# Row adds issued behind GpSimd's gate sums, and a root refined ahead of a gather, in a two-layer encoder

## Chip, cores and metric

One core of a Trainium2 chip runs the whole kernel. The metric is the device time of one execution in microseconds (us). Engines: PE is TensorE, DVE is VectorE, ACT is ScalarE, POOL is GpSimd, SP is SyncE.

## The reference, cut to what matters

Two post-norm encoder layers over 512 tokens of 1024 channels, in float32. Per layer: one input projection for two attention mixers and two sigmoid gates; each mixer's output is projected and weighted with its gate; the gated sum goes through an output projection; then a layer norm of the residual, an MLP with squared ReLU and a gated embedding, and a second layer norm.

```python
DEPTH = 2; DEEPNORM_ALPHA = (2 * DEPTH) ** 0.25
# mixer, at its end
ga, gb = jnp.split(sigmoid(gl + b_gate), 2, axis=-1)
h = einsum('bsd,de->bse', ga * ya + gb * yb, w_out)
# layer
x = layer_norm(DEEPNORM_ALPHA * x + h, ln1_g, ln1_b)
mlp = einsum('bsf,fd->bsd', square(relu(einsum('bsd,df->bsf', x, w_up))), w_down)
ple = sigmoid(einsum('bsd,de->bse', x, w_ple_gate) + b_ple_gate) * einsum('bsr,rd->bsd', p[i], w_ple)
x = layer_norm(DEEPNORM_ALPHA * x + mlp + ple, ln2_g, ln2_b)
# layer_norm(x, g, b) = (x - mean) * rsqrt(var + 1e-5) * g + b
```

## The kernel before

**Products.** A float32 factor is split into a high and a low part (`split`: ACT casts, DVE subtracts), and a product is three matmuls. Weights come packed in blocks of 512 KB from HBM through SP's queue into three staging tiles (`wst`), and are split into `whi` and `wlo` some steps ahead of PE. Line 262 is ACT's cast of all these splits and line 263 DVE's subtraction, so groups of these lines are told apart by tile.

**Gates of the second mixer, and the output projection (layer l).** For u = 0 to 3 and n = 0, 1 the loop at line 1363 takes the gate's tile t = u + 4n: PE computes the gate's projection (24 matmuls, tile `ps_('g', 1, t)`) and the branch's (6 matmuls, `yb`), ACT applies tanh (line 994), and `merged` adds: DVE forms gate times branch (line 1378), then GpSimd adds the first mixer's share (line 1380; at u = 3 DVE does it) into `hr`, of which there is one tile for all u. `mixed` splits the sum (tiles `a11h`, `axh` and their low parts), and behind n = 1 `combine` and `summed` form four more sums on DVE and split them (`smh`, `sml`). Step (u, n) below is one turn of this loop. The output projection (`Out`) and the MLP's second product (`Down`) use Strassen-like products: seven products of sums of blocks, numbered 0 to 6, each in two halves of tokens s = 0, 1; `half` is a half's 12 matmuls and `gather` adds their PSUM tile (`dn...`) into y on DVE. The sums of raw weight blocks (`raw1o`) are partly DVE's, partly accumulating DMAs issued by GpSimd (line 1260).

**The residual.** y[0] to y[3] are four tiles of 128 tokens x 1024 channels. In the second layer they are loaded from `kept` in HBM, on SP's queue (line 1370, one at each u), where the first layer left its normalised values without the norm's bias. The bias row is added afterwards by `add_row` (line 1119): a DMA issued by GpSimd that reads the row from HBM for all 128 partitions and accumulates into y[a]. It has to wait until y[a] has landed.

**Order.** PE's order is written by hand in these places. From the end of the loop (`inner`, line 1394) DVE's and ACT's is too. Elsewhere the program's scheduler orders each engine's instructions by its own forecast of when they become ready; `tc.issue_after(ins)` puts what is issued inside it behind `ins` on that engine, and `recent(engine)` is the newest instruction of that engine in the program's text. GpSimd's order is the scheduler's throughout; each engine runs its instructions in order, and one that waits holds what is behind it.

**The last norm.** In the second layer's last quarter of the MLP (q = 3) PE runs product 4, 5 and 6 by halves. `taken(n, s)` is `half` and `gather`; `moments` takes statistics of a half of y[a] (line 1011, DVE); `roots(a)` aggregates them and starts a root: a reciprocal on DVE, the square root on ACT (line 1040). What it returns, `rest()`, refines the root on DVE (four passes of one column, lines 1048 to 1075) and has ACT centre and scale y[a] (line 1078). `weighed(a)` multiplies by the norm's weight on GpSimd (line 1679) and adds y[a] to `out[a]`, where the bias row lies already, by an accumulating DMA (line 1680). out[2] is turned on PE, scaled on ACT into z and sent by SP (line 1699); out[3] is finished on DVE and sent in three pieces by SP and ACT (line 1738).

Of the kernel before, what the change touches and what calls it, by code (L numbers as in the profile page):

```python
# [17 lines left out]
DVE = mybir.EngineType.DVE  # L18
ACT = mybir.EngineType.Activation
SP = mybir.EngineType.SP  # L20

P = 128
S = 512
# [212 lines left out]
def build(nc, tc, plan, down, xw, xN, pT, wst, vec, rows, sink, cst, out):  # L236
# [3 lines left out]
    with ctx:  # L240
# [4 lines left out]
        def bank(tag, name):  # L245
            return pp.tile([P, 512], F32, tag=tag, name=name, bufs={"mm": 3, "s": 2, "pt": 2, "o": 1}[tag])
# [24 lines left out]
        def recent(engine):  # L271
            return next(i for i in reversed(nc.cur_bb.bb.instructions) if i.engine == engine)

        def in_turn(l):

            return tc.issue_after(recent(SP)) if l else ExitStack()

# [43 lines left out]
        def weights(key, look=LOOK, further=0):  # L321
            c = at[0]
            assert plan[c][0] == key, (plan[c][0], key)
            at[0] += 1
            ahead(c + look, c + further)
            return ready.pop(c)

        def mm3(ps, w, i, x, start, stop, part=False):
            s = slice(i * P, (i + 1) * P)
            nc.tensor.matmul(ps, w[0][:, s], x[0], start=start, stop=False, skip_group_check=part)  # L330
            nc.tensor.matmul(ps, w[0][:, s], x[1], start=False, stop=False, skip_group_check=part)  # L331
            nc.tensor.matmul(ps, w[1][:, s], x[0], start=False, stop=stop, skip_group_check=part)  # L332
# [59 lines left out]
        def load_vectors():  # L392
            with tc.issue_after(recent(SP)):
                nc.sync.dma_start(vraws, vec)
            nc.vector.tensor_scalar(vhs, vraws[:, :, 0:16], 0.5, None, ALU.mult)
# [595 lines left out]
        def gate(l, b, t, vt, rp, ps=None, look=LOOK):  # L991
            ps = linear((l, ("g", b, t)), X, look=look) if ps is None else ps
            g = rp.tile([P, S], F32, tag=f"gate{b}", name=f"gate{l}_{b}_{t}", bufs=2 if b else 8)
            nc.scalar.activation(g, ps, AF.Tanh, bias=vt["half"][:, b * 8 + t:b * 8 + t + 1], scale=0.5)
            return g


        class Tokens:
# [89 lines left out]
            def weighed(self, a, h):  # L1088
                c = h if isinstance(h, slice) else slice(h * 512, (h + 1) * 512)
                nc.vector.scalar_tensor_tensor(self.y[a][:, c], self.y[a][:, c], self.mv[:, a, 0:1], self.g[:, c],  # L1090
                                               ALU.subtract, ALU.mult)
# [26 lines left out]
        def add_row(y, l, i):  # L1118
            nc.gpsimd.dma_start(y, rows[l, i].partition_broadcast(P), accum_op=ALU.add)


        class Down:
# [77 lines left out]
            def product(self, q, n, then=None):  # L1200
                for s in range(2):
                    last = self.gather(q, n, s, self.half(q, n, s))
                    if then:
                        with tc.issue_after(last.ins):
                            then(s)
                return last
# [129 lines left out]
        for l in range(DEPTH):  # L1336
# [18 lines left out]
            y = [yp.tile([P, D], F32, tag=f"y{a}", name=f"y{l}_{a}", bufs=1) for a in range(4)]  # L1355
# [7 lines left out]
            for u in range(4):  # L1363
                hr = mt.tile([P, 4, 256], F32, tag="hr", name=f"hr{l}o{u}", bufs=1)
                for n, t in enumerate((u, u + 4)):
                    g = gate(l, 1, t, vt, mt, look=LOOK if u < 3 else 1 - n)
                    if not n:
                        w = weights((l, ("bb", u)), LOOK if u < 3 else 1)
                        with in_turn(l):
                            nc.sync.dma_start(y[u], kept[u] if l else xN[u])  # L1370
                        if l and u:
                            add_row(y[u - 1], l - 1, 4)
                    ps = bank("mm", f"yb{l}_{t}")
                    for i in range(2):
                        mm3(ps, w, n * 2 + i, OB[i], i == 0, i == 1)

                    def merged(u=u, n=n, t=t, g=g, ps=ps, hr=hr):
                        nc.vector.scalar_tensor_tensor(g, g, 1.0, ps, ALU.add, ALU.mult)
                        h = hr[:, 2 - 2 * n:4 - 2 * n].rearrange("p s t -> p (s t)")
                        (nc.vector if u == 3 else nc.gpsimd).tensor_tensor(h, g, ga[t], ALU.add)  # L1380
                        out7.mixed(hr, u, n)

                    if (u, n) == (3, 1):
                        break
                    merged()
                    if n:
                        out7.combine(hr)
                        out7.summed(hr, u)
                    for step in BESIDE.get((u, n), ()):
                        getattr(out7, step[0])(*step[1:])  # L1390
            manual = ExitStack()
# [5 lines left out]
            out7.cut(2, 0)  # L1397
            out7.add(3, 0)
            out7.combine(hr)
            if l:  # L1400
                add_row(y[3], l - 1, 4)
            mt_close()
            rp_close()
            np1, np1_close = pool(f"np{l}", "right")
# [4 lines left out]
            tn = Tokens(np1, y, f"n1_{l}", LN_EPS / ALPHA ** 2)  # L1409
# [39 lines left out]
            ps = product(1, 0)  # L1449
# [4 lines left out]
            ps = product(1, 1)  # L1454
# [15 lines left out]
            ps = product(4, 0)  # L1470
# [6 lines left out]
            ps = product(4, 1)  # L1477
# [5 lines left out]
            ps = product(3, 0)  # L1483
# [29 lines left out]
            ps = product(6, 0)  # L1513
# [82 lines left out]
            dn = Down(l, qp, hp, y)  # L1596
            dn.operands()
            tn = Tokens(qp, y, f"n2_{l}")
            with tc.manual_schedule(engines={PE}):
                for q in range(FQ):  # L1600
                    for i, m in enumerate(UP_ORDER):
# [3 lines left out]
                        ps = bank("mm", f"ps_up{l}_{q}_{m}")  # L1605
# [58 lines left out]
            q = FQ - 1  # L1664
            with tc.manual_schedule(engines={PE, DVE, ACT}):
                dn.cut(q, 6, 0)
                if last:
# [6 lines left out]
                    def taken(n, s, *cols):  # L1674
                        dn.gather(q, n, s, dn.half(q, n, s, *cols), *cols)
# [25 lines left out]
                    def roots(a):  # L1701
                        return tn.in_two(a, 1, root=True, centre=False)
# [8 lines left out]
                    taken(4, 1)  # L1711
                    tn.moments(1, 1)
                    rest = roots(1)
                    taken(6, 0)
                    tn.moments(2, 0)
                    rest()
                    weighed(1)
                    for n, h in ((5, 2), (6, 0)):
                        for i in range(2):
                            taken(n, 1, i * 256, i * 256 + 256)  # L1720
                            tn.moments(3, h + i, 4)
                            if h + i == 2:
                                rest = roots(2)
                            if h + i == 3:
                                rest()
# [96 lines left out]
```

## Time and profile before

| | us |
|---|---|
| median of 3 runs | 1491.35 |
| the three runs | 1489.59, 1491.35, 1491.5 |
| the profiled execution | 1491.91 |
| its span, first to last instruction | 1490.1 |
| PE busy in it | 1479.2 |
| DVE, ACT, POOL busy in it | 1074.9, 776.5, 253.8 |
| granted TensorE clock, mean | 0.998 |

The profile is of one execution. Times in it count from the span's start. A timeline's row has start, duration, engine, line, operation, out<-in, shapes, count, and in brackets the idle time of the engine before it with what ended it; a row of waits has the total, the number and the longest; the chain is the work that ended last, followed back, each step with its start and duration. In the rows by stretches each engine has its busy time and its instructions, and at the end stand the granted clock, the DMA engines' busy share and GB/s. PEld is PE's weight load, POOLq, ACTq and SPq are the engines' sequencers, q0 is the queue of GpSimd's DMAs, q1 that of SP's, q10 that of ACT's.

### The profile page before, as it was taken

The page shows a single profiled execution, that of the slowest core. Times are in us where ns is not written, and L with a number is a line of the kernel's source. Part 1 is how long each engine was busy: PE and PEld are TensorE (multiplying, and loading weights), DVE is VectorE, ACT ScalarE, POOL GpSimd, SP SyncE. Part 2 cuts the span into 40 slices and gives each one's busy share as a digit, 9 for nine tenths or more (in the row PEclk, how much of TensorE's full clock was granted, in tenths as well). Part 3 has the DMA queues.
Part 4 walks back from the last instruction along what each step waited for, and adds up shares of the span by engine and source line. Part 5 has one row for each costly group of instructions (what it writes and reads, how often), then busy time and mean ns, then how long its engine had stood idle before and what let it go on. Part 6 is the DMA issues. An engine that isn't in the chain of part 4 may idle for free.

```text
span 1490.1 us, 19508 instructions
## 1 busy us (share of the span) xinstructions
PE 1479.2 (99%) x7194; PEld 1232.3 (83%) x7194; DVE 1074.9 (72%) x1859; ACT 776.5 (52%) x1275; POOL 253.8 (17%) x223
## 2 busy tenths in 40 slices
PE   9999999999999999999999999999999999999997
PEld 8888888888888888888888888888788888888886
DVE  6766675789578777676877666756795877777768
ACT  5777764446244344444458777744462544444344
POOL 1212211110021111202012122112110202111021
PEclk9999999999999999999999999999999999999999
DMA  7656564656443414142456666548674433241503
GB/s 248 142 137 154 135 160 124 254 128 162 149 156 101 126 50 152 46 150 71 109 179 144 140 149 143 155 135 252 172 184 142 154 113 114 85 127 44 169 1 99
DMA packets 59759, 203.18 MB, mean 136 GB/s; under 512 B 7408, under 2 KB 7952, under 8 KB 59664
## 3 DMA queue, kind: packets, MB, share of 16 engines
q1 hardware_dynamic: 47120, 159.25, 32.9%
q0 software_dynamic: 11840, 42.47, 15.4%
q8 instruction: 56, 0.92, 0.2%
q10 hardware_dynamic: 704, 0.22, 0.1%
q14 instruction: 39, 0.32, 0.1%
HBM read 160.42 MB, written 6.37 MB: 112 GB/s over the span
## 4 chain that ended last, share of the span: by engine, by line
PE 90%; DVE 4%; ACT 2%; DMA 2%; issue 1%; POOL 1%; SPq 0%; DVEq 0%; POOLq 0%; ACTq 0%
PE dn L1223 20%; PE ps_up L331 8%; PE ps_up L332 8%; PE ps_up L330 8%; PE pg L337 2%; PE pg L338 2%; PE pg L336 2%; PE sa L557 1%; PE pta L520 1%; PE sb L552 1%; PE ps_start L330 1%; PE ps_start L331 1%; PE ya L330 1%; PE ps_start L332 1%; PE ya L331 1%
## 5 line engine op out<-in xcount | busy, mean ns | idle before, releaser
L262 ACT CAST whi<-wst 128x1024 fp32r<-128x1024 f32 (+1 forms) x105 | 107.1, 1020 | 211.1 <-PE ps_up L331 105.4
L330 PE MATMUL ps_up<-xhi,whi 128*128 128x512 f32 x512 | 199.2, 389 | 0.0
L331 PE MATMUL ps_up<-xlo,whi 128*128 128x512 f32 x512 | 199.2, 389 | 0.0
L332 PE MATMUL ps_up<-xhi,wlo 128*128 128x512 f32 x512 | 199.2, 389 | 0.0
L1185 POOL TENSOR_TENSOR hr<-r 128x512 f32<-128x512 f32 x64 | 104.3, 1630 | 550.0 <-ACT r L1177 529.5
L263 DVE TENSOR_TENSOR wlo<-wst,whi 128x1024 fp32r<-128x1024 f32 (+1 forms) x105 | 132.3, 1265 | 59.1 <-ACT whi L262 57.7
L1230 DVE TENSOR_TENSOR y<-y,dn 128x512 f32<-128x512 f32 (+1 forms) x114 | 76.8, 674 | 71.2 <-PE dn L1223 71.2
L330 PEld LDWEIGHTS ps_up<-xhi,whi 128*128 128x128 f32 x512 | 96.1, 188 | 20.0
L331 PEld LDWEIGHTS ps_up<-xlo,whi 128*128 128x128 f32 x512 | 96.1, 188 | 19.9
L332 PEld LDWEIGHTS ps_up<-xhi,wlo 128*128 128x128 f32 x512 | 96.1, 188 | 19.9
L262 ACT CAST whi<-raw 128x1024 fp32r<-128x1024 f32 x56 | 58.2, 1053 | 97.9 <-PE ps_up L331 54.4
L262 ACT CAST dhi<-raw 128x1024 fp32r<-128x1024 f32 x56 | 58.6, 1050 | 87.0 <-PE dn L1223 57.8
L269 POOL DMA_DIRECT2D wlo<-wst x53 | 46.6, 878 | 273.5 <-ACT wlo L268 173.2
L1165 DVE TENSOR_TENSOR raw<-raw,raw 128x1024 f32<-128x1024 f32 x64 | 84.7, 1324 | 0.5
L263 DVE TENSOR_TENSOR wlo<-raw,whi 128x1024 fp32r<-128x1024 f32 x56 | 68.3, 1220 | 11.2 <-ACT whi L262 10.1
L267 ACT CAST whi<-wst 128x1024 fp32r<-128x1024 f32 x53 | 55.5, 1048 | 29.7 <-PE ps_start L331 4.3
L263 DVE TENSOR_TENSOR dlo<-raw,dhi 128x1024 fp32r<-128x1024 f32 x56 | 68.7, 1238 | 0.4 <-ACT dhi L262 0.4
L268 ACT ACTIVATE wlo<-whi 128x1024 fp32r<-128x1024 f32 x53 | 56.2, 1061 | 0.9
L1223 PE MATMUL dn<-whi,smh 128*128 128x512 f32 (+1 forms) x130 | 50.3, 389 | 0.0
L1223 PE MATMUL dn<-whi,sml 128*128 128x512 f32 (+1 forms) x130 | 50.2, 386 | 0.0
L1223 PE MATMUL dn<-dhi,smh 128*128 128x512 f32 (+1 forms) x130 | 50.2, 386 | 0.0
L1223 PE MATMUL dn<-wlo,smh 128*128 128x512 f32 (+1 forms) x130 | 50.2, 386 | 0.0
(1219 smaller groups left out, 4079.2 us busy)
## 6 DMA issues: line engine op xcount, KB each, us to landing
wst<-wst SPq DMA_DIRECT2D x169, 512.0 KB, 3.6
raw<-wst SPq DMA_DIRECT2D x64, 512.0 KB, 4.5
wlo<-wst POOLq DMA_DIRECT2D x53, 512.0 KB, 4.9
y<-rows POOLq DMA_DIRECT2D x12, 512.0 KB, 8.4
raw0o<-wst SPq DMA_DIRECT2D x8, 512.0 KB, 11.3
raw1o<-wst SPq DMA_DIRECT2D x8, 512.0 KB, 6.3
row<-rows SPq DMA_DIRECT2D x7, 512.0 KB
xs<-xw SPq DMA_DIRECT2D x6, 512.0 KB, 6.8
```

The source lines that it names most:

```text
L262: nc.scalar.copy(hi, src)
L263: return nc.vector.tensor_tensor(lo, src, hi.bitcast(F32), ALU.subtract)
L267: nc.scalar.copy(hi, src)
L268: nc.scalar.activation(lo, hi.bitcast(F32), AF.Copy, scale=-1.0)
L269: nc.gpsimd.dma_start(lo, src, accum_op=ALU.add)
L330: nc.tensor.matmul(ps, w[0][:, s], x[0], start=start, stop=False, skip_group_check=part)
L331: nc.tensor.matmul(ps, w[0][:, s], x[1], start=False, stop=False, skip_group_check=part)
L332: nc.tensor.matmul(ps, w[1][:, s], x[0], start=False, stop=stop, skip_group_check=part)
L1165: nc.vector.tensor_tensor(to, to, other, ALU.add)
L1185: nc.gpsimd.tensor_tensor(h.rearrange("p s t -> p (s t)"), r, r, ALU.mult)
L1223: nc.tensor.matmul(ps, a[:, k, tok], w[b][:, cols], start=(first or n == 5 and c0 > 0) and not (k or m), stop=k == 3 and m == 2, skip_grou ...
L1230: done = nc.vector.tensor_tensor(to, to, ps, ALU.subtract if 1 < n < 6 else ALU.add)
```

## The change

Two edits. In the loop over the second layer's gates the four adding DMAs of the bias row are issued at other places. Before, y[u - 1]'s was issued right behind the load of y[u] at step (u, 0) for u = 1 to 3, and y[3]'s after the loop. Now y[u - 1]'s is issued behind the merging of step (u, 0), and behind the newest GpSimd instruction at that point, and at u = 3 y[2]'s and y[3]'s both. In the last norm the second `rest()`, with `weighed(1)`, comes between the matmuls of product 6's first half and their gather; before, it came behind that gather and the statistics of it.

```diff
+POOL = mybir.EngineType.Pool
...
                         with in_turn(l):
                             nc.sync.dma_start(y[u], kept[u] if l else xN[u])
-                        if l and u:
-                            add_row(y[u - 1], l - 1, 4)
                     ps = bank("mm", f"yb{l}_{t}")
...
                     if n:
                         out7.combine(hr)
                         out7.summed(hr, u)
+                    elif l and u:
+                        with tc.issue_after(recent(POOL)):
+                            for a in range(u - 1, u + u // 3):
+                                add_row(y[a], l - 1, 4)
...
             out7.combine(hr)
-            if l:
-                add_row(y[3], l - 1, 4)
             mt_close()
...
                     taken(4, 1)
                     tn.moments(1, 1)
                     rest = roots(1)
-                    taken(6, 0)
-                    tn.moments(2, 0)
+                    ps = dn.half(q, 6, 0)
                     rest()
                     weighed(1)
+                    dn.gather(q, 6, 0, ps)
+                    tn.moments(2, 0)
                     for n, h in ((5, 2), (6, 0)):
```

## The prediction

> **What bounds the kernel now.** I read the page's busy shares first, then the table by stretches, then TensorE's (PE's) waits, then the chain that ended last around the two edited places, then the timelines of the engines there. PE is busy for 99% of the span, which ends at 1490.1 us, so only the time in which PE does not stream can be won. The stretches (columns: PE, PE weight loads, VectorE = DVE, ScalarE = ACT, GpSimd = POOL, granted clock, DMA share, GB/s):
>
> ```profile
> PE 1479.2 (99%) x7194; PEld 1232.3 (83%) x7194; DVE 1074.9 (72%) x1859; ACT 776.5 (52%) x1275; POOL 253.8 (17%) x223
> ...
> 1000.00:1046.92 46.92, 46.92 (x208) 38.86 (x207) 29.32 (x37) 18.04 (x24) 10.87 (x8) 1.00 0.80 256
> 1046.92:1104.80 57.88, 57.10 (x246) 45.51 (x245) 51.35 (x78) 29.33 (x34) 8.71 (x9) 1.00 0.65 168
> 1104.80:1480.90 376.10, 376.09 (x1696) 312.02 (x1695) 280.97 (x366) 161.92 (x209) 61.72 (x41) 1.00 0.34 105
> 1480.90:1490.10 9.20, 1.31 (x8) 0.84 (x8) 5.02 (x14) 4.00 (x11) 0.89 (x1) 0.68 0.68 176
> ```
>
> PE has no gap at all in the first half of the second layer's gates (to 1046.92) nor in the whole MLP behind it (1104.8 to 1480.9). It has gaps between 1046.92 and 1104.8, the last gates and the out projection, and it is nearly done in the last 9.2 us, which are the last norm and its transfers. The two edits lie in just these two places.
>
> How much PE loses between the gates and the norm is more than its idle 0.78 us, because a busy matmul may start late. I take it from starts:
>
> ```profile
> 1006.12 0.39 PE L330 MATMUL ps_('g', 1, 0)_9333<-xhi,whi 128*128 128x512 f32 x1
> ...
> 1011.56 0.39 PE L330 MATMUL yb<-obh,whi 128*128 128x512 f32 x1
> ...
> 1046.92 0.39 PE L330 MATMUL ps_('g', 1, 3)_9661<-xhi,whi 128*128 128x512 f32 x1
> ...
> 1104.85 0.40 PE L338 MATMUL ple<-whi,pl 128*128 128x512 f32 x1
> ```
>
> The first two rows are 24 matmuls apart in a stretch without gaps: 5.44 / 24 = 0.2267 us from start to start. The last two rows have 247 starts between them: 247 x 0.2267 = 56.0 us, against 57.93 us taken. PE loses 1.93 us here. For what:
>
> ```profile
> PE ps_('g', 1, 7)_9713 L332 <- DVE wlo L263: 0.4, 1, 0.4
> PE dn_-1_0_0_9787 L1223 <- DVE y L1313: 0.2, 1, 0.2
> ...
> PEld ps_('g', 1, 7)_9713 L332 <- DVE wlo L263: 0.8, 1, 0.8
> PEld dn_-1_0_0_9787 L1223 <- ACT dhi1o L1282: 0.6, 1, 0.6
> ```
>
> These rows are waits (total, times, longest). Each is for DVE or for ACT, which make weight halves or gather sums: the vector side is late here, not the weights from HBM. The chain says why it is late:
>
> ```profile
> 1039.24 7.87 DMA y<-kept
> 1047.15 0.60 issue
> 1047.77 0.89 POOL y L1119
> 1048.65 1.33 POOL hr1o L1380
> ...
> 1052.50 2.21 DVE wlo L263
> ...
> 1074.31 4.56 DMA raw1o<-raw1o
> ```
>
> Line 1119 is `add_row`. The load of y[3] was issued at 1039.24 and took 7.87 us; GpSimd stood at the adding DMA of that row until 1047.77, with the gates' sum (line 1380) queued behind it. From there the chain goes through ACT to the `wlo` that PE waits for.
>
> **Part 1, the second layer's adding DMAs.** Nothing is added or removed in number: four DMAs with 0.88 to 0.9 us of GpSimd each, before and after. Moved: y[0]'s behind the sum of step (1,0), y[1]'s behind that of (2,0), y[2]'s and y[3]'s together behind the newest GpSimd instruction at (3,0), which is the sum of (2,1), since at u = 3 the sum is DVE's. They move past sums on GpSimd's queue alone; SP's queue, with the loads of y and the weights, keeps its order.
>
> These are rows of DVE, ACT and GpSimd around the wait (start, duration, in brackets the idle time before), the issues of the row adds by their durations in ns, and the time that the four adds in question took to land:
>
> ```profile
> 1044.06 1.22 DVE L263 TENSOR_TENSOR sml<-hr1o,smh 128x1024 fp32r<-128x1024 f32 x1
> ...
> 1050.01 0.41 ACT L262 CAST a11h<-hr1o 128x256 fp32r<-128x256 f32 x1 [6.59 <-POOL hr1o L1380]
> ...
> 1047.77 0.89 POOL L1119 DMA_DIRECT2D y<-rows  x1 [10.02 <-DMA y<-kept]
> 1048.37 1.60 POOL L1380 TENSOR_TENSOR hr1o<-gate,gate 128x512 f32<-128x512 f32 x1
> 1052.34 1.29 POOL L1380 TENSOR_TENSOR hr1o<-gate,gate 128x512 f32<-128x512 f32 x1 [2.36 <-DVE gate L1378]
> ...
> 1077.30 0.67 DVE L1313 SCALAR_TENSOR_TENSOR y<-dn_-1_2_0_9872,y 128x512 f32<-128x512 f32 x1
> ...
> L1119 POOL DMA_DIRECT2D y<-rows x6: 877/888/1150, 1007.3 to 1107.9; - x6
> ...
> DMA to landing us min/median/max: 5.1/8.8/9.2
> ```
>
> - The sum of (2,0) needs `hr`, free when DVE's `sml` ends: 1044.06 + 1.22 = 1045.3. It started at 1048.37. Without the row add ahead of it, it starts some 3.1 us earlier, and ends at about 1046.6 (1.29 us, the shorter of the two rows) instead of 1049.97. ACT stood 6.59 us for it and comes 3.1 to 3.4 us forward.
> - ACT's next cast writes a buffer that PE reads until about 1047.1 (the gate after it starts at 1046.92), so what follows on ACT moves by some 3.2 us (it was at 1050.3). The sum of (2,1), then `wlo` of gate (1,7), follow by the same amount: `wlo` ends near 1051.5 instead of 1054.7. PE waited 0.4 us for it and so wanted it at 1054.3: the first wait goes, with 2.8 us to spare.
> - From there DVE works through a queue that is 51.35 of 57.88 us busy. It is late at PE's other stops, by less than a microsecond each. With DVE 3 us ahead and PE ahead by at most 1.93, these stops go too. What is late next is PE itself.
> - The adds after their move: y[1]'s stands ahead of the sum of (2,1) but is issued right behind (2,0), at about 1046.6 to 1047.9, while that sum waits for DVE until about 1049: covered. y[2]'s and y[3]'s are issued at about 1050.4 to 1052.5; even with 9.2 us each, one after the other, they land by 1071. The first user of y[2] is the gather at 1077.30, at about 1074 after the move. Covered by 3 us; if that cover were gone, the price is one for one on DVE's queue.
>
> Bounds for this part: at the least the one wait that the chain ends in, 0.4 us; at the most the whole 1.93. I take 1.9, as a shift of 3.1 us is larger than anything it has to cover.
>
> **Part 2, the second root of the last norm.** The order of PE's instructions is the same. On DVE four passes of one column go ahead of a gather and its statistics; nothing is added or removed.
>
> ```profile
> 1474.54 0.20 ACT L1040 ACTIVATE nsmn<-nsmn 128x1 f32<-128x1 f32 x1 [0.43 <-DVE nsmn L1039]
> 1475.09 0.69 DVE L1230 TENSOR_TENSOR y<-y,dn 128x512 f32<-128x512 f32 x1 [0.58 <-PE dn L1223]
> 1476.43 0.20 DVE L1048 TENSOR_SCALAR nsmn<-nsmn 128x1 f32<-128x1 f32 x1
> 1477.29 0.41 DVE L1230 TENSOR_TENSOR y<-y,dn 128x256 f32<-128x256 f32 x1
> 1477.41 1.52 ACT L1078 ACTIVATE y<-y,nsmn 128x512 f32<-128x512 f32 x2 [2.66 <-DVE nsmn L1075]
> 1476.44 0.90 POOL L1680 DMA_DIRECT2D out<-y  x1 [0.41 <-POOL y L1679]
> 1478.31 2.54 POOL L1679 TENSOR_TENSOR y<-y,row 128x512 f32<-128x512 f32 x2 [0.98 <-ACT y L1078]
> 1481.26 0.89 POOL L1680 DMA_DIRECT2D out<-y  x1 [0.41 <-POOL y L1679]
> ```
>
> ACT's root is there at 1474.74. DVE now stands idle 0.58 us for PE and refines only at 1476.43. After the change the four passes (1476.43 to 1477.29, 0.86 us) run at about 1474.8 to 1475.66, mostly in that idle time; gather and statistics (1475.09 to 1476.43, 1.34 us) follow until 1477.0, and the next gather is 0.3 us earlier than 1477.29. So nothing behind is delayed. ACT's pass on y[1] moves from 1477.41 to about 1475.8. GpSimd cannot follow all the way: it issues out[0]'s DMA until 1476.44 + 0.90 = 1477.34. Its passes start there instead of 1478.31, and out[1]'s adding DMA moves 0.97 us, from 1481.26 to 1480.3.
>
> Does that reach the end? The last column of these rows is GB/s, the one before it the DMA share; the queue row is that of the window 1484 to 1485, in which it is the only queue:
>
> ```profile
> 1482.50:1483.00 0.50, 0.07 (x1) 0.00 (x0) 0.50 (x2) 0.50 (x3) 0.00 (x0) 1.00 1.29 131
> ...
> 1487.00:1488.00 1.00, 0.00 (x0) 0.00 (x0) 0.00 (x0) 0.00 (x0) 0.00 (x0) 0.50 1.05 392
> ...
> 1488.50:1489.00 0.50, 0.00 (x0) 0.00 (x0) 0.00 (x0) 0.00 (x0) 0.00 (x0) 0.50 0.11 37
> ...
> q0 software_dynamic: 41, 0.17, 87.0%
> ...
> 1483.58 0.33 SPq L1699 DMA_DIRECT2D out<-z  x1
> ```
>
> From 1482.5 until 1488.5 the 16 DMA engines are nearly full. First out[1]'s adding DMA fills them alone: the first half of out[2] was issued at 1483.58 and has no packet before 1485. Then come out[2] and out[3]. The tail is a queue behind out[1], so an earlier out[1] ends it earlier, by 0.97 us at most; at the least by nothing, if the last pieces of out[3] take their time from their own issue. I take 0.8, near the upper end, as the engines have little free time between the two.
>
> What speaks against this part is the row of issues above: one took 1.15 us instead of the 0.88 of the shortest, which would take 0.27 from the gain. The Trainium skill's page "SBUF — State Buffer", section "SBUF: two separate sides", goes further: a DVE pass in a two-port mode keeps GpSimd from writing the descriptors of its DMAs, 620 ns growing to some 3100. By that rule, as an estimate, out[1] would leave 2.5 us later and this part would be a loss of 1.5 us. The trace does not show it: the out issues took 0.90 and 0.89 us, the first of them with the DVE passes of 1476.43 to 1477.29 beside it.
>
> **Sum.** 1.9 + 0.8 = 2.7 us off. The profiled execution took 1491.91 us (its span of 1490.1 and 1.8 around it), so 1489.2; it stands 0.56 us above the median of the three runs (1491.35), and set against that median the forecast is 1488.65, told as 1488.7: 0.18% less.
>
> **The rivals.**
> - *Only the first wait goes.* The out projection's vector queue is paced by the sums of raw weights that arrive by DMA (the chain row of 4.56 us at 1074.31), so the 3 us are lost there; and out[3]'s own issue sets the end. For it: PE waits just 0.4 + 0.2 us by name. Against: those DMAs are issued when DVE has cut, so they move with it. Gain 0.4 to 1.0 us: 1490.4 to 1490.9.
> - *The edits do nothing at the end.* The wait comes back at another place, for instance at y[2]'s and y[3]'s adds in one burst, which share the engines with the weights for the next stage, and the tail stays: 1491.3. For it: an add takes up to 9.2 us to land. Against: the 3 us of cover at the gather, and the tail's full engines.
> - *Slower: a new order on ACT and DVE.* In the gates' stage and in the MLP these two engines are ordered by the scheduler's own forecast, which is run anew with GpSimd's changed queue. If it puts a weight's cast behind one that waits for GpSimd, PE stands: the wait of 6.59 us that ACT had here cost PE 0.4, so 6.2 us were covered; to end 3 us above the old time a wait must cost PE 2.7 + 3 = 5.7 us, and so be near 12 us long, or fall in several places. It would show as PE idle in the MLP, where 0.01 us is idle now. Time: 1494.4 from that point on, say to 1496.
> - *GpSimd's issue of out[1] drawn out beside DVE.* By 0.27 us on the rows above: 1488.9, inside the forecast's own range. By the estimate from the Trainium skill's page "SBUF — State Buffer" it would be a loss in the tail of 1.5 us, and the time near 1491.
>
> **How the numbers follow.** Chances: forecast 0.60, only the first wait 0.22, nothing 0.09, slower 0.07, the issue drawn out so far that the tail's gain is lost 0.02. The range runs from 1487.6 (both parts at their upper ends, 2.9 us, with the runs' scatter of about 1 us) to 1491.4 (the case "nothing"). About 0.2%, 3.0 us, is what a measurement of this kernel can tell from no change. The forecast's 2.7 is just under it, so of its 0.60 I give 0.32 to faster by more than that, from the scatter, and 0.28 to within; the next two cases and the last lie within; slower gets 0.07. In all 0.32, 0.61, 0.07.
>
> **What would show it.** In the changed kernel's timeline GpSimd's sum of (2,0) starts near 1045.4, with the row adds behind it; `wlo` of gate (1,7) ends before 1052; the PE waits at gate (1,7) and at the out projection are gone and PE's stretch behind 1046.92 is 1.9 us shorter; the last norm has its second refinement at about 1474.8 less those 1.9; out[1]'s DMA leaves about 1 us earlier relative to PE's last matmul, and the DMA engines fall silent about 0.8 us earlier behind it. The prediction is wrong if PE's waits reappear in other lines, if PE idles in the MLP, or if the silence at the end keeps its distance from PE's last matmul.

## The result, and the profile after

The changed kernel takes 1488.84 us (median of 22 runs; before 1491.4 us, median of 22): a ratio of 0.9985 with a 95% interval of 0.9978 to 0.9991, 2.6 us less by the medians. The ratio is not that of the two medians: it stands for 2.2 us, and its interval for 1.3 to 3.3. The forecast was 1488.7, with 2.7 us less.

In the execution that was profiled first (3020.59 us) PE ran at half its usual pace throughout, so the profile shown here is of another execution of the same instructions (run `both_parts`, 1488.16 us); there POOL is defined in the line of SP, so only the loop's lines differ from before: 1376 is the gate times the branch (1378 before), 1378 the sum (1380 before).

First PE's time from the first matmul of gate (1,3) to the first transpose of the norm, 246 matmuls in both (the counts in the rows take in those that reach over an edge); the first number behind the window is its length, the next PE's busy time in it. Before:

```profile
1046.92:1105.09 58.17, 57.40 (x248) 45.67 (x247) 51.64 (x78) 29.33 (x34) 8.71 (x9) 1.00 0.66 169
```

and after, with PE's waits in the whole span:

```profile
1046.33:1102.10 55.77, 55.77 (x248) 46.13 (x246) 52.30 (x80) 29.44 (x34) 9.09 (x11) 1.00 0.76 191
...
PE warm L256 <- DVE rgap L252: 1.0, 1, 1.0
PE ob L561 <- DVE ogb L567: 0.7, 2, 0.4
PE oa L562 <- DVE ptla L263: 0.3, 2, 0.2
```

246 x 0.2267 = 55.77 us: PE now loses nothing here, and both waits of this stretch are gone from the list. What it lost before was 58.17 - 55.77 = 2.40 us.

GpSimd and DVE around the place, after (start, duration, idle before in brackets), and how the four row adds landed:

```profile
1045.05 1.29 POOL L1378 TENSOR_TENSOR hr1o<-gate,gate 128x512 f32<-128x512 f32 x1 [10.00 <-DVE sml L263]
1046.28 0.88 POOL L1119 DMA_DIRECT2D y<-rows  x1
1048.72 1.28 POOL L1378 TENSOR_TENSOR hr1o<-gate,gate 128x512 f32<-128x512 f32 x1 [1.55 <-DVE gate L1376]
1049.94 1.81 POOL L1119 DMA_DIRECT2D y<-rows  x2
...
1048.86 2.22 DVE L263 TENSOR_TENSOR wlo<-wst,whi 128x1024 fp32r<-128x1024 f32 x1 [0.24 <-ACT whi L262]
...
1073.73 0.69 DVE L1313 SCALAR_TENSOR_TENSOR y<-dn_-1_2_0_9872,y 128x512 f32<-128x512 f32 x1
...
DMA to landing us min/median/max: 5.7/7.8/10.2
```

The sum of (2,0) now waits for DVE's `sml` and no longer for a load. `wlo` of gate (1,7) ends at 1051.08, 4.75 us behind the start of gate (1,3) (1046.33); before it was 7.79 us (1054.71 less 1046.92).

The last norm after, on ACT, DVE and GpSimd:

```profile
1471.53 0.20 ACT L1040 ACTIVATE nsmn<-nsmn 128x1 f32<-128x1 f32 x1 [0.42 <-DVE nsmn L1039]
1471.76 0.21 DVE L1048 TENSOR_SCALAR nsmn<-nsmn 128x1 f32<-128x1 f32 x1 [0.27 <-ACT nsmn L1040]
1472.64 0.68 DVE L1230 TENSOR_TENSOR y<-y,dn 128x512 f32<-128x512 f32 x1
1472.76 1.52 ACT L1078 ACTIVATE y<-y,nsmn 128x512 f32<-128x512 f32 x2 [1.03 <-DVE nsmn L1075]
1473.42 0.90 POOL L1680 DMA_DIRECT2D out<-y  x1 [0.41 <-POOL y L1679]
1474.04 2.86 POOL L1679 TENSOR_TENSOR y<-y,row 128x512 f32<-128x512 f32 x2
1477.31 0.89 POOL L1680 DMA_DIRECT2D out<-y  x1 [0.41 <-POOL y L1679]
```

The end is measured from the start of PE's last product matmul, 1480.61 before and 1477.51 after. From there to the end of the span:

```profile
1480.61:1490.10 9.49, 1.59 (x11) 0.92 (x9) 5.27 (x15) 4.29 (x11) 1.13 (x2) 0.69 0.69 175
```

```profile
1477.51:1486.40 8.89, 1.59 (x11) 0.92 (x9) 5.18 (x14) 4.12 (x11) 0.69 (x1) 0.78 0.78 190
...
1484.50:1485.00 0.50, 0.00 (x0) 0.00 (x0) 0.00 (x0) 0.00 (x0) 0.00 (x0) 0.50 0.86 295
1485.00:1485.50 0.50, 0.00 (x0) 0.00 (x0) 0.00 (x0) 0.00 (x0) 0.00 (x0) 0.50 0.04 12
```

The first row is before, the others are after: 0.60 us less. A span's end is printed to 0.1 us, so each tail is known to some 0.05. out[1]'s DMA, issued 0.65 us behind that matmul before, is issued 0.20 us ahead of it. Hardly a packet starts later than 7.5 us behind it (1485.0), and the last one ends at 7.63 us; before, it ended at 8.29.

Between the two stretches, from the first transpose of the norm to that last product matmul, PE takes 375.41 us (1477.51 less 1102.10) and took 375.52 (1480.61 less 1105.09). Some 0.1 us of it lie where product 6 begins its second half, before and after:

```profile
1477.76 0.38 PE L1223 MATMUL dn<-whi,axh 128*128 128x256 f32 x1
1477.98 0.28 PE L1223 MATMUL dn<-wlo,axh 128*128 128x256 f32 x1
```

```profile
1474.75 0.28 PE L1223 MATMUL dn<-whi,axh 128*128 128x256 f32 x1
1474.87 0.28 PE L1223 MATMUL dn<-wlo,axh 128*128 128x256 f32 x1
```

The two starts are 0.12 us apart now and were 0.22 apart; they are 0.21 to 0.22 apart in every profile of this study with the second root late, and 0.12 in every one with it early. This matmul adds into the bank that DVE's gather of product 5 reads (1477.29 to 1477.70 before); that gather, counted from the first transpose, now comes 0.34 us earlier (371.86 instead of 372.20).

So the two traces differ by 2.40 us in the gates and the out projection, by 0.11 behind them and by 0.60 in the tail, 3.1 in all; the spans differ by 3.7, as gate (1,3) itself began 0.6 us later in the execution profiled before. The medians say 2.6. The starts of gate (1,3) lie between 1046.33 and 1048.36 in the profiles of this study, so a median of a single edit is known to some tenths only, and the stretches of the trace say more.

### The profile page after: what moved, and what is told of

Same layout as the page of the kernel before. It is cut to its first block, busy times and chain, and to the rows that moved or that the text cites. A ratio compares the mean times of both kernels' runs of the same rounds, so it can differ in the third digit from the quotient of the medians.

```text
span 3018.8 us, 19508 instructions
## 1 busy us (share of the span) xinstructions
PE 3011.5 (100%) x7194; PEld 1977.5 (66%) x7194; DVE 1082.8 (36%) x1859; ACT 783.6 (26%) x1275; POOL 249.8 (8%) x223
## 4 chain that ended last, share of the span: by engine, by line
PE 100%; DVE 0%; DVEq 0%; issue 0%
PE dn L1224 21%; PE ps_up L331 8%; PE ps_up L333 8%; PE ps_up L332 8%; PE pg L338 2%; PE pg L339 2%; PE pg L337 2%; PE pta L521 1%; PE sa L558 1%; PE sb L553 1%; PE ya L331 1%; PE ya L333 1%; PE ps_start L333 1%; PE ps_start L331 1%; PE ps_start L332 1%; PE ya L332 1%
## 5 line engine op out<-in xcount | busy, mean ns | idle before, releaser
L331 PE MATMUL ps_up<-xhi,whi 128*128 128x512 f32 x512 | 345.5, 675 | 0.0
L333 PE MATMUL ps_up<-xhi,wlo 128*128 128x512 f32 x512 | 345.4, 675 | 0.0
L332 PE MATMUL ps_up<-xlo,whi 128*128 128x512 f32 x512 | 345.0, 674 | 0.0
L333 PEld LDWEIGHTS ps_up<-xhi,wlo 128*128 128x128 f32 x512 | 152.9, 299 | 87.3 <-issue 81.6
L331 PEld LDWEIGHTS ps_up<-xhi,whi 128*128 128x128 f32 x512 | 152.5, 298 | 86.7 <-issue 79.5
L332 PEld LDWEIGHTS ps_up<-xlo,whi 128*128 128x128 f32 x512 | 152.1, 297 | 86.5 <-issue 80.5
L1224 PE MATMUL dn<-whi,sml 128*128 128x512 f32 (+1 forms) x130 | 88.4, 680 | 0.0
L1224 PE MATMUL dn<-dlo,smh 128*128 128x512 f32 (+1 forms) x130 | 88.0, 677 | 0.0
L1224 PE MATMUL dn<-whi,smh 128*128 128x512 f32 (+1 forms) x130 | 86.5, 669 | 0.0
L1224 PE MATMUL dn<-dhi,sml 128*128 128x512 f32 (+1 forms) x130 | 85.3, 656 | 0.0
```

The lines of the kernel that those rows point to most:

```text
L1224: nc.tensor.matmul(ps, a[:, k, tok], w[b][:, cols], start=(first or n == 5 and c0 > 0) and not (k or m), stop=k == 3 and m == 2, skip_grou ...
```

## The experiments

All of them are against the kernel before on the same chip. The theory: in the gates GpSimd's stand at the row adds is PE's loss, and in the tail all waits for out[1]'s transfer. The rivals are these: only one wait is won and the rest stays; the gain comes from another order of DVE; out[3]'s own issue sets the end.

**1. The whole change again** (`both_parts`). The edit is the change itself.

> The changed kernel once more, for a profile at the usual clock. Theory (PE's loss in the last gates and the out projection goes, and the tail ends earlier): 2.7 us less than before; PE takes 1.9 us less from the start of gate (1,3) to the step in front of the norm, and the engines fall silent 0.8 us sooner behind PE's last matmul. Rival (only the first wait goes): 0.4 to 1.0 us less, with PE still waiting at the out projection.

Measured: 1488.47 us against 1491.31, ratio 0.9983 (0.9975 to 0.9992). The stretches were shown above: 2.40 instead of 1.9, 0.60 instead of 0.8. The rival falls, as no wait is left in the out projection.

**2. The row adds alone** (`rows_only`): the first part of the diff without the second.

> Only the four row adds are moved, the last norm is as before. Theory: 1.9 us less than before, all of it between the start of gate (1,3) and the first norm. Rival: 0.4 us, the first wait alone. If the tail gives nothing by itself, this kernel equals the whole change.

Measured: 1489.64 us, ratio 0.9990 (0.9981 to 0.9999), 1.7 us less. The stretches, gates and out projection first, tail second:

```profile
1047.12:1102.89 55.77, 55.77 (x247) 46.13 (x246) 52.23 (x80) 28.91 (x33) 8.52 (x10) 1.00 0.76 192
...
1478.41:1488.00 9.59, 1.59 (x11) 0.91 (x9) 5.28 (x15) 4.29 (x11) 1.16 (x2) 0.67 0.69 172
```

All of PE's loss is gone, and the tail is what it was (9.59 beside 9.49).

**3. The second root alone** (`root_only`): the second part of the diff without the first.

> Only the second root is refined ahead of the gather, the row adds are as before. Theory (the tail is a queue of transfers behind out[1]'s): 0.8 us less than before, out[1]'s DMA issued about 1 us earlier. Rival (out[3]'s own issue sets the end): 0 to 0.1 us less with out[1] 1 us earlier all the same.

Measured: 1490.63 us, ratio 0.9995 (0.9986 to 1.0004), 0.7 us less; by the interval alone it could be none.

```profile
1046.51:1104.57 58.06, 57.39 (x247) 45.67 (x246) 51.63 (x78) 29.34 (x34) 8.71 (x9) 1.00 0.66 167
...
1479.98:1488.80 8.82, 1.59 (x11) 0.92 (x9) 5.17 (x14) 4.11 (x11) 0.67 (x1) 0.85 0.79 192
...
1047.27 0.89 POOL L1119 DMA_DIRECT2D y<-rows  x1 [10.05 <-DMA y<-kept]
```

The loss stays at 58.06 - 55.77 = 2.29 us, and the tail is 0.67 us shorter than before. Between the two PE takes 375.41 us, as with the whole change; with the row adds alone it took 375.52. The parts' stretches add up: nothing is seen to be won or lost by making both. The medians, 1.7 + 0.7 us against 2.8, agree with that within their intervals.

**4. y[3]'s add alone** (`y3_only`). Moving all four adds lets the scheduler change DVE's order in three places: a sum of raw blocks goes two steps ahead, a product with a gate and a cut one step each. With y[3]'s alone, this one DMA's place on GpSimd is all that differs from before:

```diff
                     merged()
+                    if u == 2:
+                        gates_sum = recent(POOL)
...
+                    elif l and u == 3:
+                        with tc.issue_after(gates_sum):
+                            add_row(y[3], l - 1, 4)
...
-            if l:
-                add_row(y[3], l - 1, 4)
```

> Of the four row adds only y[3]'s is moved behind GpSimd's sum of (2,1); y[0]'s to y[2]'s stay, and no other engine's order differs from before. Theory (it is GpSimd's stand at y[3]'s load that costs the time): 1.7 to 1.9 us less than before, nearly all that moving the four gives. Rival (the gain comes from the other adds, or from the order on DVE that the scheduler changes when all four are moved): less than 0.5 us.

Measured: 1489.47 us, ratio 0.9987 (0.9978 to 0.9996), 1.8 us less.

```profile
1046.09 1.29 POOL L1380 TENSOR_TENSOR hr1o<-gate,gate 128x512 f32<-128x512 f32 x1 [9.07 <-DVE sml L263]
...
1050.97 0.89 POOL L1119 DMA_DIRECT2D y<-rows  x1
...
1046.36:1102.48 56.12, 56.12 (x248) 45.99 (x246) 51.64 (x78) 29.43 (x34) 8.34 (x9) 1.00 0.69 175
```

Of the 2.40 us, 58.17 - 56.12 = 2.05 go with this one add. The other three and DVE's order account for 0.35.

**5. The early root with out[1] held back** (`held_out1`). The root is refined early, but GpSimd's passes on y[1] stand behind a one-column copy that waits for statistics of y[3]; the row adds are as before:

```diff
+                    ps = dn.half(q, 6, 0)
                     rest()
-                    weighed(1)
+                    dn.gather(q, 6, 0, ps)
+                    tn.moments(2, 0)
...
                             if h + i == 2:
+                                hold = nc.gpsimd.tensor_copy(wgap[:, :1], tn.st[:, 3, 2, :1])
+                                with tc.issue_after(hold.ins):
+                                    weighed(1)
```

> The second root is refined ahead of the gather as in the change, but GpSimd's passes on y[1], and with them out[1]'s DMA, are held until DVE has the first statistics of y[3], by a one-column copy on GpSimd; the row adds are as before. Theory (the tail's gain is out[1]'s earlier transfer): the gain is gone, the time is that of the kernel before within 0.2 us, about 9.5 us from PE's last product matmul to the end. Rival (the gain comes from DVE's own order): still 0.6 to 0.7 us less, about 8.85 us.

Measured: 1491.06 us against 1491.66, ratio 0.9997 (0.9988 to 1.0006).

```profile
1048.36:1106.46 58.10, 57.43 (x247) 45.66 (x246) 51.66 (x78) 29.37 (x34) 8.73 (x9) 1.00 0.65 166
...
1481.87:1491.30 9.43, 1.59 (x11) 0.91 (x9) 5.18 (x14) 4.12 (x11) 0.96 (x2) 0.77 0.71 179
...
1049.10 0.89 POOL L1119 DMA_DIRECT2D y<-rows  x1 [9.55 <-DMA y<-kept]
...
1482.35 0.89 POOL L1680 DMA_DIRECT2D out<-y  x1 [0.41 <-POOL y L1679]
```

out[1]'s DMA is issued 0.48 us behind PE's last product matmul again, and the tail is back at 9.43, while DVE's order is the early one. The tail's gain is out[1]'s. In front of the tail PE takes 375.41 us here too (1481.87 less 1106.46), and the two starts of product 6 are 0.12 us apart. So the 0.1 us that PE wins there are DVE's order: the rival holds for that much. The median lies 0.6 us below that of before, more than the 0.2 expected; that 0.1 us is part of it, and the rest, with an interval across 1, I count as scatter.

**6. Without out[1]'s DMA** (`no_out1`), on the kernel before: `weighed` issues the adding DMA for a = 0 only.

> The kernel before without out[1]'s adding DMA; out[1] keeps only the bias row. It shows how much the tail owes to that transfer at all. Theory: out[2] and out[3] start as soon as they are issued, and the end comes 1.0 to 1.2 us earlier, from 9.5 to about 8.4 us behind PE's last product matmul. Rival (out[3]'s last issue sets the end): no change, 9.4 to 9.5 us.

Measured: 1491.01 us against 1491.66, ratio 0.9995 (0.9986 to 1.0004).

```profile
1047.42:1106.33 58.91, 57.48 (x248) 45.59 (x247) 51.64 (x78) 29.38 (x34) 8.72 (x9) 1.00 0.66 169
...
1481.81:1490.30 8.49, 1.59 (x11) 0.91 (x9) 5.28 (x15) 4.31 (x11) 0.25 (x1) 0.75 0.40 135
...
1049.00 0.88 POOL L1119 DMA_DIRECT2D y<-rows  x1 [10.27 <-DMA y<-kept]
```

The tail is 8.49, 1.00 us shorter: that is all out[1] can cost, and the change has 0.60 to 0.75 of it. Why the median fell by 0.65 only is not shown. The profiled execution is the slowest of the eleven (1492.07), and in it PE lost 58.91 - 55.77 = 3.14 us at the gates. With runs 3 and 5, where the row adds are as before too, this makes a scale that nobody set: y[3]'s add began 0.74, 0.76, 0.85 and 1.58 us after the start of gate (1,3) (runs `held_out1`, `root_only`, before, `no_out1`), and PE lost 2.33, 2.29, 2.40 and 3.14 us. From the first three to the fourth, each 0.1 us by which the load of y[3] came later cost PE about 0.1 us; as the three lie close together, this is in the main one comparison.

**7. No row adds at all** (`no_rows`): the changed kernel without the four.

> The changed kernel without the second layer's four row adds; the first layer's last bias is missing from the residual. Theory (behind the gates' sums the adds are fully covered): the same as the changed kernel within 0.2 us, 2.4 to 2.8 us less than before. Rival (their transfers or issues still hold up the out projection): 0.5 us or more below the changed kernel.

Measured: 1488.68 us against 1491.66, ratio 0.9981 (0.9972 to 0.9990), 3.0 us less.

```profile
1047.49:1103.26 55.77, 55.77 (x248) 46.13 (x246) 51.71 (x79) 28.05 (x32) 6.50 (x7) 1.00 0.63 165
...
1478.74:1487.60 8.86, 1.59 (x11) 0.91 (x9) 5.17 (x14) 4.12 (x11) 0.72 (x1) 0.82 0.76 188
```

The stretches are those of the changed kernel, 55.77 and 8.86. Behind the sums the adds cost nothing that shows.

**8 and 9. Both roots early** (`both_roots`, and again beside the changed kernel). The first root too is refined ahead of a gather:

```diff
-                    taken(5, 0)
-                    tn.moments(2, 1)
+                    ps = dn.half(q, 5, 0)
                     rest()
                     weighed(0)
+                    dn.gather(q, 5, 0, ps)
+                    tn.moments(2, 1)
```

> The changed kernel with the first root too refined ahead of a gather, that of product 5's first half. Theory: out[0]'s DMA leaves about 0.9 us earlier and GpSimd is free sooner, so out[1]'s leaves about 0.6 us earlier than in the changed kernel; the tail gives another 0.3 to 0.4 us, and the whole is 2.9 to 3.2 us less than before. Rival (the tail is at the bound of out[3]'s own issue by now): the same as the changed kernel within 0.1 us.

> The changed kernel beside the version with both roots early, on one chip. Theory and rival alike: 2.5 to 2.9 us less than before; the tail 8.8 to 8.9 us behind PE's last product matmul.

> Both roots refined ahead of a gather, beside the changed kernel. Theory (its profile had the tail 0.4 us shorter, 8.46 against 8.89, with nothing else changed): 0.4 us less than the changed kernel, 2.9 to 3.3 less than before. Rival (0.4 us in one profile does not carry to the median): within 0.1 us of the changed kernel.

Measured: 1488.63 us against 1491.66, ratio 0.9981 (0.9972 to 0.9989), 3.0 us less as the first theory had it; on one chip with the changed kernel 1488.39 against its 1488.28 (before: 1491.11; ratios 0.9982, 0.9973 to 0.9991, and 0.9981, 0.9973 to 0.9990). The tail of the second pair, both roots early:

```profile
1478.44:1486.90 8.46, 1.59 (x11) 0.92 (x9) 5.24 (x14) 4.22 (x11) 0.10 (x1) 0.87 0.74 186
...
1469.58 0.39 PE L1223 MATMUL dn<-dhi,sml 128*128 128x512 f32 x1
1469.99 0.47 PE L1223 MATMUL dn<-whi,axh 128*128 128x512 f32 x1
1470.29 0.40 PE L1223 MATMUL dn<-wlo,axh 128*128 128x512 f32 x1
...
1469.16 0.68 DVE L1230 TENSOR_TENSOR y<-y,dn 128x512 f32<-128x512 f32 x1
```

and the changed kernel beside it:

```profile
1478.16:1486.90 8.74, 1.59 (x11) 0.91 (x9) 5.17 (x14) 4.11 (x11) 0.68 (x1) 0.87 0.77 191
...
1467.93 0.67 DVE L1230 TENSOR_TENSOR y<-y,dn 128x512 f32<-128x512 f32 x1
```

The tail is 0.28 us shorter than the changed kernel's (0.4 was foretold) and, with 8.46 us, at the 8.49 us that run 6 left without any out[1]. But the spans are equal, since PE stops: the first starts of its product 6 come 0.41 and 0.30 us apart instead of 0.23. This product adds into the bank of product 5, which the gather has to read first, and that gather, now behind the refinement, ends at 1469.84 instead of 1468.60. PE comes to its tail 0.25 us later. The second root could be put ahead because no product waits for the gather that it delays; of the first root that does not hold. It is no better than the change: its median lies 0.11 us above, and the theory of 0.4 us less falls.

## Why the prediction was right

- **The cause in the gates.** GpSimd's stand at y[3]'s load held the sum of (2,0), and through it ACT and DVE: shown by run 4, which moves that one add and changes nothing else. The sum's start was foretold as 1045.4, 3.1 us earlier, and came at 1045.05; measured from gate (1,3) it went from 1.45 us behind that gate's start (1048.37 less 1046.92) to 1.28 us ahead of it (1046.33 less 1045.05), which is 2.73 us earlier. `wlo` of gate (1,7) came 3.04 us earlier by the same measure (4.75 us behind instead of 7.79).
- **Its size** was the term that was mis-sized: 1.9 foretold, with 1.93 as the upper bound, and 2.40 measured. The failing step is the count of starts: it said 247 between the two rows, and there are 245. 245 x 0.2267 = 55.54, and 57.93 - 55.54 = 2.39. The reasoning that all of it would go was right.
- **Covered adds.** y[2]'s and y[3]'s were issued at 1049.94 (foretold 1050.4) and landed within 10.2 us each; the gather of y[2] was at 1073.73 (foretold 1074). Run 7 shows that they cost nothing.
- **The tail.** 0.8 was foretold. The four profiles of changed tails (8.74 to 8.89) are 0.60 to 0.75 shorter than that of before, and 0.70 to 0.85 shorter than the unchanged tail of run 2 (9.59), so 0.8 is within what these profiles allow. On GpSimd out[1]'s DMA followed out[0]'s by 3.89 us, as foretold (3.86; before 4.82). That it came forward by 0.85 us and not by 0.97 against PE's last product matmul is in the main that matmul's own doing, which came 0.11 us earlier behind the first transpose. That the tail is a queue behind out[1] was right (run 5), up to a bound that the prediction did not have: 1.00 us, when out[1] is gone (run 6).
- **DVE's delay** of the gather did not show, as foretold: the next gather came 0.34 us earlier (0.3 foretold). The prediction took nothing from that, but PE won some 0.1 us by it, since a product waited for that gather's bank. It looked at DVE's queue alone; what also has to hold is that no product of PE waits for the bank that the delayed gather reads, as runs 8 and 9 show.
- **The rivals.** "Only the first wait" and "nothing" fall with run 2. The scheduler did make a new order on DVE, in the three places named at run 4; it cost nothing that can be seen, as PE's stretch is without loss. ACT's order is that of before. GpSimd's issues of the out DMAs took 0.90 and 0.89 us after the move too. So no delay shows by the rule of the Trainium skill's page "SBUF — State Buffer", section "SBUF: two separate sides", by which a DVE pass in a two-port mode keeps GpSimd from writing descriptors; whether a DVE pass beside these issues was in such a mode, no run shows.
- **The total.** That 1.9 + 0.8 = 2.7 fell so near the measured 2.6 is in part luck: the one term was too small by 0.5, PE's 0.1 us behind the out projection was not foreseen, and the profiled execution stood 0.5 us above its median. The traces' own difference is 3.1.

## What to carry to other kernels

An instruction that only issues a transfer still holds its engine's queue while it waits for its operand, so put it behind the short work that others wait for, not at the first place where it may go. Look for it where the chain passes from a load through an issuing engine to a sum that does not use that load. When small work is put ahead of a gather from PSUM, look first who waits for that bank: with no product behind it the move cost nothing, and with one it cost as much as it won.

## What the runs showed of the hardware that was not expected

The first half of out[2], issued by SP, had no packet beside GpSimd's adding DMA of out[1] until that was nearly through. In the profile before its first packet came 1.87 us behind its issue and 0.83 us ahead of the end of out[1]'s last; in run `no_out1`, without out[1]'s DMA, it came 0.83 us behind its issue. There the tail was 1.00 us shorter (8.49 against 9.49).

A wait that the list of PE's waits gives as 0.4 and 0.2 us was worth 2.05 to 2.40 us of PE, though PE is shown as busy for nearly all of it: only the starts, 0.2267 us apart where nothing is lost, tell what a stretch loses.
